# Reading back the reciprocals of a pair of heads: one transfer for both heads, or one transfer per head

## The chip, the cores and the metric

The kernel runs on one core of one Trainium2 chip. The metric is the device time of one execution in microseconds (us); lower is better. The core has a matrix engine (PE in the profile, with its weight loads as PEld), a vector engine (DVE), a scalar engine (ACT), a general engine (POOL) and a sync engine (SP). SP, ACT and POOL can issue DMA transfers; the packets of all transfers are moved by the core's 16 DMA engines.

## The reference

One layer of a streaming encoder over 1024 positions with a width of 1024, all in float32. Two kinds of attention stand side by side, each with 8 heads of 64 columns, and a gated feed-forward block follows. Cut to what matters here:

```python
o_a = from_heads(forgetting_attention(qa, ka, va, log_f))      # 8 heads, strictly causal, with a decay
o_b = from_heads(chunk_band_attention(qc, kc, vc, rel_bias))   # 8 heads, band of 8 chunks back, with a bias
merged = sigmoid(g_A) * (o_a @ w_branch_a) + sigmoid(g_B) * (o_b @ w_branch_b)
x = x + merged @ w_out
x = x + square(relu(rms_norm(x) @ w_up)) @ w_down
return rms_norm(x)
```

Inside both attentions the weights are a softmax: `p = exp(logit - max) / sum(exp(logit - max))`, then `p @ v`. The division by the sum is what this case is about.

## The kernel before, in words

**Stages.** First come the norm and the projections (queries, keys, values and gates; Strassen products of 512-column blocks), to about 430 us of the profile. Then the 16 heads of attention are run one after the other, to about 720 us. Then come the branch products, the output projection, the feed-forward up and down, and the final norm. The matrix engine takes float32 data as a rounded high part and a low part, so that a product is three matmuls; ACT makes the high part, DVE or POOL the low part.

**The attention stage.** The heads are taken in pairs, `pr` = 4, 5, 6, 7 (the forgetting heads), then 0, 1, 2, 3 (the band heads). `hh` is the head within the pair, `h` the half of the 1024 queries. The order of work is written out by hand: strings of letters (`FOX_HEAD`, `BAND_HEAD`, `LAST_HEAD`) name one action each. `S` makes the scores of one block of 128 queries on PE (tile `s`, from the loaded tiles `qk` and `sk`), `R` takes their extremum on DVE (band heads add the loaded bias tile `bc` there), `E` takes the exponential on ACT (tile `p`, with the row sums added up into `den`), `T` turns `p` on PE (`pt`), `H` and `L` make the high and low part (`th` on ACT, `tl` on DVE), `P` multiplies with the loaded values `v` (`pv`), `V` and `X` bring the result out. `F` is one step of a filler: parts of the gated branch products (tile `m`), with weights `wrab`, `wh_ab` and `wl_ab`, which PE runs between attention work in the later heads. `O` and `W`, in the last head alone, split reloaded outputs `olt` (ACT, then DVE) and the first branch weights. The engines' wrappers `TO`, `VO`, `AO` and `LO` keep these instructions in the order of the letters on PE, DVE, ACT and SP; instructions of the bare POOL object `G`, and the bare engines elsewhere, are placed by a planner, which works with modelled times.

**Loads.** All loads of the stage are issued by SP in one order (`LO`). When the scores of a head are done, the tiles `qk` (1 MB) and `sk` (512 KB) of the head after next are loaded into the buffers that this head leaves (`load_head`); `load_bias` and `load_values` do so for `bc` and `v`. So a load has about the time of one head before PE needs it.

**The reciprocals.** The row sums of a pair stand in `den` with one query in each partition. `reciprocals(pr)` inverts them, transposes them in blocks of 32 and writes them to `r_dram[pr]`, a tensor of 2 rows (one for each head) of 1024 floats, in four small transfers. The output tile `on` has the 64 columns of the pair's first head in partitions 0 to 63 and those of the second in partitions 64 to 127, and queries along the free axis. `spread_reciprocals(pr)` therefore reads each row of `r_dram[pr]` into 64 partitions of the tile `rb`, 128 partitions of 4 KB in all, and `normalise` multiplies `on` by `rb`: on POOL (line 860) for seven of the eight pairs, on DVE for the last (pair 3). For the band pairs the product is stored to `o_dram` by SP (the store waits in the list `later` for the next `flush`) and reloaded as `olt`. `spread_reciprocals` is called from `done`, between the two halves of the queries of a pair's second head.

Of the kernel before, what the change touches and what calls it, by code (L numbers as in the profile page):

```python
# [19 lines left out]
S = 1024  # L20
# [3 lines left out]
HD = 64  # L24
# [67 lines left out]
def hybrid_block(ctx: ExitStack, tc: tile.TileContext, xT, xN, g1, wall, wf, fb, relb, g2, g3, outT):  # L92
# [14 lines left out]
    VO, TO, AO, GO, LO = Ordered(V), Ordered(T), Ordered(A), Ordered(G), Ordered(nc.sync)  # L107
# [29 lines left out]
    def dram(name, shape, dt=F32):  # L137
        return dpool.tile(shape, dt, tag=name, name=name)
# [5 lines left out]
    r_dram = dram("r_dram", [8, 2, S])  # L144
# [702 lines left out]

    def spread_reciprocals(pr):
        rb = ap0.tile([P, S], F32, tag="rb", name=f"rb{pr}")
        LO.dma_start(rb, r_dram[pr].rearrange("a (o s) -> a o s", o=1).to_broadcast([2, HD, S]))  # L850
        outs["rb", pr] = rb

    def normalise(pr, h):
# [46 lines left out]
    def done(n, h):  # L900
        pr, hh = HEADS[n]
        flush()
        if n == 15:
            if h == 0:
                spread_reciprocals(pr)
            else:
                normalise(pr, h)
        elif hh:
            if h == 0:
                o = outs[pr, h]  # L910
                G.tensor_tensor(o, o, lows_o[pr], op=ALU.add)
                spread_reciprocals(pr)
            normalise(pr, h)
# [420 lines left out]
```

## Time and profile before

| what | value |
|---|---|
| median of 3 runs | 1477.45 us (1476.58 to 1478.12) |
| the profiled execution | 1475.98 us |
| its span, first to last instruction | 1474.3 us |
| busy: PE, DVE, ACT, POOL | 96%, 60%, 48%, 55% of the span |
| mean granted PE clock | 0.980 |
| data moved by DMA | 259.75 MB, mean 176 GB/s |
| first and last issue of an `rb` transfer | 448.1 us and 697.1 us |

The profile is of one execution. The profile's page gives shares over the whole span; answers for chosen stretches give the busy time of each engine, the granted clock of PE, the share of the 16 DMA engines that was busy and the rate. A wait is put down to what came last, and the chain is followed back from the last instruction to what released each step. The time of a DMA in the chain runs from its issue to its landing.

### The profile page before, as it was taken

The numbers are of one execution on the slowest core, as the hardware profiler recorded it, in microseconds if no ns is written. First come the engines' busy times: TensorE is split into PE (matmuls) and PEld (weight loads), VectorE is DVE, ScalarE is ACT, GpSimd is POOL, SyncE is SP. The second block draws the span as 40 slices with busy tenths as digits, with TensorE's granted clock in tenths as the row PEclk, the third lists the DMA queues.
The fourth block names the chain that finished last, engine by engine and source line by source line (L and its number), as shares of the span: only waits on it lengthen the run. The fifth ranks groups of instructions, "written<-read, shape, count | busy, mean of one in ns | idle before, by whom it ended". The sixth has DMA issues, their size and how long they took to land.

```text
span 1474.3 us, 20382 instructions
## 1 busy us (share of the span) xinstructions
PE 1415.2 (96%) x6658; PEld 1176.5 (80%) x6658; DVE 890.9 (60%) x1385; ACT 707.9 (48%) x1363; POOL 816.0 (55%) x641
## 2 busy tenths in 40 slices
PE   7999999999989888989899999999999999999997
PEld 5788888888877777878688888888888888888886
DVE  7756454533368876656546674555455558999644
ACT  8633333344358776656335443333333444444654
POOL 1477777777802222112453487777776645658463
PEclk9999999999999989989999999999999999999998
DMA  8547667763355576885555334444444875578363
GB/s 275 153 113 199 182 193 216 200 192 133 131 176 157 135 199 172 216 221 194 188 195 169 115 111 147 157 150 157 155 151 139 279 240 173 165 255 222 93 206 123
DMA packets 132580, 259.75 MB, mean 176 GB/s; under 512 B 18354, under 2 KB 20402, under 8 KB 129402
## 3 DMA queue, kind: packets, MB, share of 16 engines
q1 hardware_dynamic: 84618, 173.32, 38.6%
q10 hardware_dynamic: 44656, 77.26, 16.6%
q0 software_dynamic: 3200, 7.88, 2.4%
q8 instruction: 52, 0.85, 0.2%
q14 instruction: 54, 0.44, 0.1%
HBM read 172.70 MB, written 85.69 MB: 175 GB/s over the span
## 4 chain that ended last, share of the span: by engine, by line
PE 73%; DMA 15%; DVE 5%; issue 4%; POOL 1%; ACT 1%; SPq 1%; POOLq 0%; ACTq 0%; DVEq 0%
PE u L215 42%; PE dS L215 8%; PE dA L215 7%; PE o L215 5%; DMA sk<-sk_dram 4%; DMA bc<-relb 3%; PE m L215 3%; PE s L105 2%; DMA rb<-r_dram 2%; PE pv L105 2%; PE pt L105 2%; DMA wr<-wall 2%; DMA xT<-a_dram 1%; DMA v<-v_dram 1%; PE u L105 1%
## 5 line engine op out<-in xcount | busy, mean ns | idle before, releaser
L164 POOL TENSOR_TENSOR wl_A<-wr,wh_A 128x512 fp32r<-128x512 f32 x118 | 157.6, 1345 | 90.2 <-ACT wh_A L162 74.0
L164 POOL TENSOR_TENSOR wl_S<-S,wh_S 128x512 fp32r<-128x512 f32 x102 | 136.5, 1342 | 30.7 <-ACT wh_S L162 30.1
L162 ACT CAST wh_S<-S 128x512 fp32r<-128x512 f32 x105 | 64.7, 621 | 116.9 <-PE u L215 53.7
L105 DVE TENSOR_TENSOR tl<-pt,th 128x512 fp32r<-128x512 f32 (+1 forms) x144 | 90.8, 642 | 31.5 <-ACT th L105 30.0
L162 ACT CAST wh_A<-wr 128x512 fp32r<-128x512 f32 x105 | 64.9, 620 | 86.6 <-PE u L215 47.7
L164 POOL TENSOR_TENSOR wl_S<-ks,wh_S 128x512 fp32r<-128x512 f32 x48 | 70.9, 1565 | 51.9 <-ACT wh_S L105 50.2
L105 ACT CAST th<-pt 128x512 fp32r<-128x512 f32 (+1 forms) x144 | 77.3, 550 | 41.5 <-PE pt L105 39.1
L105 ACT ACTIVATE p<-s,mn 128x640 f32<-128x640 f32 (+3 forms) x120 | 84.2, 702 | 22.0 <-DVE mn L105 21.1
L578 DVE TENSOR_TENSOR u<-u,u 128x512 f32<-128x512 f32 x70 | 48.8, 697 | 74.1 <-PE u L215 71.8
L860 POOL TENSOR_TENSOR on<-on,rb 128x512 f32<-128x512 f32 x14 | 17.7, 1275 | 127.3 <-DMA rb<-r_dram 127.3
L105 PE MATMUL pt<-ident,p 128*128 128x128 f32 x528 | 82.0, 284 | 0.7 <-DVE zt L391 0.6
L185 POOL TENSOR_TENSOR S<-wr,wr 128x512 f32<-128x512 f32 x35 | 46.5, 1328 | 61.1 <-DMA wr<-wall 47.1
L105 PEld LDWEIGHTS pt<-ident,p 128*128 128x128 f32 x528 | 65.0, 146 | 11.2 <-PE pv L105 2.0
L105 PE MATMUL s<-qk 128*128 128x384 f32 (+2 forms) x192 | 60.7, 371 | 13.2 <-DMA qk<-qk_dram 6.6
L105 PE MATMUL s<-sk 96*128 96x384 f32 (+2 forms) x192 | 55.5, 343 | 11.3 <-DMA sk<-sk_dram 11.3
L164 POOL TENSOR_TENSOR wl_A<-ka,wh_A 128x512 fp32r<-128x512 f32 x32 | 46.1, 1449 | 35.2 <-ACT wh_A L105 35.2
L105 PE MATMUL pv<-th,v 128*128 128x512 f32 (+3 forms) x180 | 62.7, 356 | 1.1 <-ACT th L105 0.5
L277 ACT CAST qkh<-qk 128x512 fp32r<-128x512 f32 x32 | 19.9, 621 | 88.4 <-DMA qk_dram<-qkl 34.1
L1089 ACT ACTIVATE v<-v 128x512 f32<-128x512 f32 x64 | 40.4, 632 | 45.3 <-DVE v L1088 43.4
L105 DVE CUSTOM_DVE_ANT_0 s<-s,bc 128x640 f32<-128x640 f32 (+2 forms) x64 | 42.3, 662 | 32.6 <-DMA bc<-relb 18.5
L571 DVE TENSOR_TENSOR u<-u,c 128x512 f32<-128x512 f32 x35 | 24.5, 699 | 55.8 <-PE u L215 53.8
L105 PE MATMUL pv<-tl,v 128*128 128x512 f32 (+3 forms) x180 | 57.7, 339 | 0.2 <-DVE tl L105 0.2
(441 smaller groups left out, 4725.2 us busy)
## 6 DMA issues: line engine op xcount, KB each, us to landing
wr<-wall SPq DMA_DIRECT2D x235, 256.0 KB
a_dram<-at ACTq DMA_DIRECT2D x64, 256.0 KB
xT<-a_dram SPq DMA_DIRECT2D x64, 256.0 KB
qk<-qk_dram SPq DMA_DIRECT2D x15, 1024.0 KB
qk_dram<-qkh ACTq DMA_DIRECT2D x96, 128.0 KB
a_dram<-v ACTq DMA_DIRECT2D x48, 256.0 KB
xB<-a_dram SPq DMA_DIRECT2D x44, 256.0 KB
z_dram<-zt ACTq DMA_DIRECT2D x32, 256.0 KB
```

Source lines behind the costliest of these rows:

```text
L105: return lambda *a, **kw: tc.keep_in_program_order(getattr(self.eng, name)(*a, **kw))
L162: (act.tensor_copy if act is G else act.copy)(wh, src)
L164: lows.append(eng.tensor_tensor(wl, src, wh.bitcast(F32), op=ALU.subtract))
L185: eng.tensor_tensor(t, raw(3), raw(2), op=ALU.add)
L215: done = eng.matmul(bank, w[wi], x[xi], start=(first and t == 0), stop=(t == n - 1 and not part), skip_group_check=part or not first)
L277: A.copy(dst[0], src)
L571: V.tensor_tensor(banks[1], banks[3], c22, op=ALU.add)
L578: V.tensor_tensor(banks[b], banks[b], u2, op=ALU.add)
L860: G.tensor_tensor(o, o, rb, op=ALU.mult)
L1089: A.activation(v, v, AF.Square)
```

## The change

The one transfer that filled all 128 partitions of `rb` becomes two in a loop over the heads of the pair, of 64 partitions each. Source bytes, destination bytes, the issuing queue and the place in SP's order stay the same. The source of the old transfer is a three-dimensional pattern, 2 rows by 64 repeats by 1024 floats; that of each new one is 64 repeats by 1024 floats.

```diff
     def spread_reciprocals(pr):
         rb = ap0.tile([P, S], F32, tag="rb", name=f"rb{pr}")
-        LO.dma_start(rb, r_dram[pr].rearrange("a (o s) -> a o s", o=1).to_broadcast([2, HD, S]))
+        for hh in range(2):
+            LO.dma_start(rb[hh * HD:(hh + 1) * HD, :], r_dram[pr, hh:hh + 1, :].to_broadcast([HD, S]))
         outs["rb", pr] = rb
```

## The prediction

> **What bounds the kernel now.** I read the page first: the busy times, the chain, the group of line 860.
>
> ```profile
> PE 1415.2 (96%) x6658; PEld 1176.5 (80%) x6658; DVE 890.9 (60%) x1385; ACT 707.9 (48%) x1363; POOL 816.0 (55%) x641
> PE 73%; DMA 15%; DVE 5%; issue 4%; POOL 1%; ACT 1%; SPq 1%; POOLq 0%; ACTq 0%; DVEq 0%
> L860 POOL TENSOR_TENSOR on<-on,rb 128x512 f32<-128x512 f32 x14 | 17.7, 1275 | 127.3 <-DMA rb<-r_dram 127.3
> ```
>
> PE is busy for 96% of the span, so a gain must come out of its 59 us of idle time or out of a slowed clock. The chain holds 15% of DMA. POOL waits 127.3 us for `rb`, seven times, 18 us each: for 512 KB that is long. Next, the chain in order of time, which gives the transfers of the attention stage from issue to landing, and the PE stretch that follows the stage:
>
> ```profile
> 452.75 16.50 DMA sk<-sk_dram
> 484.00 17.43 DMA sk<-sk_dram
> 550.13 21.04 DMA sk<-sk_dram
> 625.67 17.06 DMA rb<-r_dram
> 715.99 39.05 PE m L215 x163
> ```
>
> The `sk` load issued at 452.75 needs 16.5 us, though only one `rb` transfer (448.05) stands ahead of it and its neighbours. Why is seen in busy time by windows, whose last columns are the PE clock, the share of the 16 DMA engines and the rate:
>
> ```profile
> 449.10:452.10 3.00, 3.00 (x17) 2.56 (x16) 2.84 (x8) 2.00 (x5) 0.00 (x0) 1.00 0.12 46
> 452.90:460.00 7.10, 6.40 (x46) 5.71 (x46) 5.99 (x16) 6.66 (x16) 0.00 (x0) 1.00 0.95 237
> 462.80:464.00 1.20, 1.20 (x8) 0.97 (x8) 1.20 (x4) 1.19 (x3) 0.00 (x0) 1.00 0.14 48
> 584.90:587.00 2.10, 2.10 (x16) 1.96 (x15) 1.88 (x5) 1.37 (x3) 0.00 (x0) 1.00 0.10 29
> 676.00:679.00 3.00, 3.00 (x20) 2.64 (x18) 2.78 (x7) 2.15 (x6) 0.00 (x0) 1.00 0.14 55
> ```
>
> While `rb` is alone in flight (first row), 0.12 of 16 engines are busy: two, at 23 GB/s each. With the loads behind it, all are busy (0.95). By 462.8 the share is back at 0.14, while `sk` lands at 469.25: the other 14 engines have done their part, and the load waits for its share on the two that still carry `rb`. The last two rows show the same in other pairs. So each `rb` transfer makes two engines late by 7 to 10 us, and everything issued behind it is as late as they are.
>
> [...]
>
> What this costs PE: its waits in the stage, then the stretches that hold them (engine columns PE, PEld, DVE, ACT, POOL), and last the sum of the eight stretches between these.
>
> ```profile
> PE s L105 <- DMA sk<-sk_dram: 11.3, 6, 2.3
> PE s L105 <- DMA qk<-qk_dram: 6.6, 4, 3.4
> PE m L215 <- ACT wh_ab L105: 5.2, 1, 5.2
> PE m L105 <- POOL wl_ab L745: 5.1, 3, 4.2
> PE pv L105 <- DMA v<-v_dram: 0.5, 1, 0.5
> ```
>
> ```profile
> 467.16:474.14 6.98, 4.74 (x24) 4.08 (x24) 4.14 (x15) 3.95 (x11) 3.50 (x4) 0.76 0.94 262
> 498.19:504.87 6.68, 3.61 (x16) 3.53 (x17) 2.85 (x9) 3.37 (x8) 4.51 (x5) 0.74 0.94 256
> 530.14:542.41 12.27, 8.06 (x31) 7.12 (x32) 5.15 (x16) 5.33 (x14) 6.78 (x7) 0.58 0.72 200
> 565.35:576.54 11.19, 5.62 (x16) 4.54 (x17) 2.03 (x5) 2.30 (x7) 7.29 (x7) 0.70 0.80 241
> 607.30:612.10 4.80, 2.75 (x14) 1.99 (x13) 0.76 (x3) 1.54 (x5) 0.84 (x1) 1.00 0.99 320
> 642.40:655.05 12.65, 6.40 (x17) 4.81 (x17) 2.24 (x6) 2.61 (x7) 4.98 (x4) 0.60 0.72 245
> 709.40:719.90 10.50, 5.15 (x12) 3.64 (x12) 5.02 (x5) 3.38 (x6) 4.66 (x3) 0.68 0.39 124
> sum 65.07, PE 36.33 PEld 29.70 DVE 22.19 ACT 22.48 POOL 32.56; mean PE 5.19 PEld 4.24 DVE 3.17 ACT 3.21 POOL 4.65
> ...
> sum 206.08, PE 202.24 PEld 175.50 DVE 159.34 ACT 152.65 POOL 27.43; mean PE 25.28 PEld 21.94 DVE 19.92 ACT 19.08 POOL 3.43
> ```
>
> Seven stretches, one near the end of each head or pair that has an `rb` transfer in flight, hold 65.07 us with only 36.33 us of PE work. And the clock falls: 0.58 to 0.76 in six of the seven, which are those with the longest waits, against 1.00 in the one with short waits. Between them PE is busy 202.24 of 206.08 us, 98.1%, at full clock.
>
> **The change, part by part.** *More engines.* Each half has 64 rows of 4 KB, four per engine if it uses 16. At the 23 GB/s per engine of the lone transfer, 512 KB on 16 engines take 1.4 us; at the full load's 237 GB/s, 2.2 us. A fixed part comes on top, for which this row of the chain, a write of 2 KB, gives a bound of 2.8 us:
>
> ```profile
> 622.70 2.83 DMA r_dram<-rt
> ```
>
> So `rb` lands 4 to 5 us after its issue instead of 16 to 17 (up to 8 where loads stand ahead). POOL's waits fall from 127.3 us to 7 x 5 = 35, which is worth nothing in itself except where POOL delays PE. Loads behind it lose the wait for two late engines and pay at most 2.2 us for the bytes that now go over their engines too. `sk` of the first pair, issued at 452.75, should land by 462, when the other engines were done (0.14 at 462.8); PE wants it at 467.16, 5 us later. That margin is the cover of the remaining cost.
>
> *One more issue.* Eight more DMA instructions on SP, each new one priced by loads of 64 rows:
>
> ```profile
> L105 SPq DMA_DIRECT2D rb<-r_dram x8: 533/540/578, 448.1 to 697.1; - x8
> L105 SPq DMA_DIRECT2D sk<-sk_dram x12: 455/465/1442, 452.8 to 651.9; - x12
> L105 SPq DMA_DIRECT2D bc<-relb x16: 465/578/963, 515.8 to 653.2; - x16
> ```
>
> Two issues of 0.46 to 0.58 instead of one of 0.54 add 0.4 to 0.6 us per pair, 3 to 5 us on SP in all. In the first pair the next issues come at 452, 3.4 us after `rb`, and hide it. Where loads follow at once (the last pair's `olt`), they go out 0.5 us later, and land earlier all the same. Without that cover it would be 8 x 0.5 = 4 us; I take 0.3 us per pair, 2.4. POOL waits for two transfers instead of one; the second wait costs one semaphore check, 17 ns by this row, eight times, under other waiting:
>
> ```profile
> L860 POOLq EVENT_SEMAPHORE  x8: 17/17/17, 464.1 to 680.8; - x8
> SPq L105 <- POOL on L860: 38.8, 3, 13.2
> ACT oh L105 <- DMA olt<-o_dram: 11.1, 1, 11.1
> ```
>
> *What moves with it.* SP stands 38.8 us behind line 860 for the stores to `o_dram`, with weight loads queued behind them. POOL waits for `rb` ahead of `wl_ab`, for which PE then waits 4.2 us. In the last head ACT waits 11.1 us for `olt`, issued right behind `rb`, and `wh_ab`, for which PE waits 5.2 us, stands behind that on ACT. All three shrink with `rb`.
>
> *The sum.* Idle time in the seven stretches: 65.07 - 36.33 = 28.7 us. Clock: the lost share, (1 - clock), times the length of each sums to 20.4 us; times PE's busy time instead to 11.4. Slow clock over idle time costs nothing, over work everything; I take the middle, 15.9. The work of these stretches at full clock is then 36.33 - 15.9 = 20.4 us, and at the 98.1% of the other stretches 20.8. Upper bound of the saving: 65.07 - 20.8 = 44.3.
>
> Next late: ACT. The first three pair periods and a wait-free stretch:
>
> ```profile
> 448.05:479.80 31.75, 28.81 (x173) 24.91 (x174) 25.62 (x59) 25.85 (x61) 7.61 (x7) 0.95 0.57 151
> 479.80:511.70 31.90, 28.14 (x171) 24.67 (x169) 25.11 (x58) 25.22 (x59) 7.59 (x7) 0.95 0.57 150
> 511.70:546.47 34.77, 29.87 (x166) 25.76 (x164) 24.66 (x57) 24.79 (x57) 9.39 (x9) 0.85 0.65 167
> 474.14:498.19 24.05, 23.37 (x146) 20.12 (x144) 20.76 (x43) 21.18 (x48) 3.07 (x3) 1.00 0.47 122
> ```
>
> ACT has 75.9 us of work in these three pairs. Bound by PE alone they would take some 82 us, with ACT at 92%; its best sustained share here is 21.18 of 24.05, 88%, which gives 86.2. That takes 4.1 back. 44.3 - 4.1 - 2.4 = 37.8 us. The profiled execution took 1475.98, 1.5 below the median of the runs: 1476.0 - 37.8 = 1438.
>
> It reaches the end, because the stretch after the stage is PE work without a gap (39.05 us in the chain) and later weight loads start when buffers come free, earlier too.
>
> **The rivals.** *Part of it only.* The waits for `sk`, `qk` and `v` go (11.3 + 6.6 + 0.5 = 18.4) but the clock stays as it is, ACT takes its 4.1 and SP 2.4: 12 us, 1464; with a third of the rest about 1455. For it: the reason for the slow clock is seen only by its place beside the waits. Against: 1.00 in the one stretch whose waits are short.
>
> *No gain.* Two halves are two transfers over the same engines with the fixed part paid twice, and what PE waits for is late for another reason: 1476, or 1480 with all of SP's 4 us. Against: engines stand idle (0.14) while `sk` is awaited. [...]
>
> [...]
>
> *Slower by the source row.* Sixteen engines read one row of 4 KB at once. If a row gives its 23 GB/s however many read it, a half takes 11.4 us, both 22.8 one after the other, with all engines held: everything behind lands 9 us later than now, in six places about 54 us, 1530. It decides where both halves need over 16.5 us, below 38 GB/s from one row. For it: nothing here reads a row with 16 engines. Against: one engine's 23 GB/s on one row is above the 15 GB/s (237 / 16) that each gets under full load, so the row is not what limits.
>
> **How the numbers follow.** Forecast 0.74, part of it 0.14, no gain 0.06, no change from two engines 0.01, and slower 0.05 (source row 0.03, one engine 0.02). The forecast alone spans 1427 (the clock's upper bound, 20.4, and nothing taken back: 65.07 - 15.9 / 0.981 = 48.9) to 1450. Down to 1428 and up to 1463, which takes in most of "part of it", leaves out about 2 in 10. Measurements tell some 0.2%, 3 us, from no change: faster 0.88, same 0.07, slower 0.05.
>
> **What would show it.** Right: with `rb` alone in flight the DMA share is near 0.9 for 2 us instead of 0.12; line 860 waits some 35 us in place of 127; `sk` lands 8 to 9 us after issue; the clock keeps 1.00 through most of the stage; PE's waits for `qk` and `sk` nearly vanish; the stage ends 35 to 40 us sooner and the rest has its old length. Wrong: a share of 0.06 or 0.12 again, or waits of PE on ACT that grow by as much as the DMA waits shrink.

## The result, and the profile after

The changed kernel takes 1433.28 us (median) against 1477.78 us before, a ratio of 0.9695 (95% interval 0.9675 to 0.9714). Measured again with another set of runs it takes 1432.24 against 1478.67 us, 0.9681 (0.9657 to 0.9705). That is 44.5 and 46.4 us saved, where 38 were forecast. In the profiled execution of the first measurement, one of the four runs in the 1433.28, PE was slow from end to end (7217 us), so every line of "after" below comes from the second measurement, whose profiled span is 1430.6 us.

The page after, in the lines that answer to those of before (busy times; the chain; and, from the list of all groups of instructions, POOL's multiplication, now on line 861):

```profile
PE 1397.9 (98%) x6658; PEld 1165.7 (81%) x6658; DVE 884.8 (62%) x1385; ACT 706.5 (49%) x1363; POOL 813.5 (57%) x641
PE 83%; issue 4%; DVE 4%; POOL 3%; ACT 2%; DMA 2%; SPq 0%; POOLq 0%; ACTq 0%; DVEq 0%
L861 POOL TENSOR_TENSOR on<-on,rb 128x512 f32<-128x512 f32 x14 | 17.8, 1287 | 42.0 <-DMA rb<-r_dram 42.0
```

DMA's part in the chain falls from 15% to 2%. Between 440 and 760 us the DMA steps of 16 to 21 us quoted before are gone: the chain there is PE work for 93%, and no DMA stands in it. POOL waits 42.0 us for `rb` where it waited 127.3, 6 us each.

Busy time by windows: `rb` alone in flight, the loads behind it, and the time in which before only two engines were left at work.

```profile
450.60:452.40 1.80, 1.80 (x10) 1.50 (x9) 1.80 (x4) 0.85 (x4) 0.00 (x0) 1.00 0.97 250
454.40:461.00 6.60, 5.91 (x43) 5.19 (x42) 5.29 (x15) 6.18 (x17) 6.09 (x6) 1.00 0.94 299
463.00:465.00 2.00, 2.00 (x14) 1.73 (x13) 2.00 (x5) 1.99 (x6) 0.00 (x0) 1.00 0.00 0
```

The share of the 16 DMA engines (last column but one) is 0.97 where it was 0.12, and by 463 us, where two engines went on alone before, nothing is left to move.

The traces also note the landing of each transfer in 16 parts. Six `sk` loads of the stage are issued right behind an `rb` transfer. Before, 14 of the 16 parts of such a load were there 8.6 to 11.5 us after its issue, and the last two came 7.5 to 12 us later, so that the load landed after 16.5 to 22.1 us. Now all 16 parts are there after 7.3 to 9.3 us in four of the six and after 11.0 and 12.9 us in the other two (8 to 9 were forecast). That a part is one engine's share is the author's reading; it agrees with two late parts at a share of 0.12 here and four at 0.26 in the run on four engines below.

All waits of PE in the attention stage, in sum, times, and the longest:

```profile
PE s L105 <- ACT p L105: 5.7, 9, 0.9
PE s L105 <- DVE tl L105: 0.2, 1, 0.2
```

The waits for `sk`, `qk`, `wh_ab`, `wl_ab` and `v` are all gone. Last, the attention stage as a whole, from the first `rb` issue to the start of the last high part of `o3h`, before and then after, in one row each:

```profile
448.05:719.90 271.85, 238.59 (x1360) 205.23 (x1361) 182.22 (x403) 175.65 (x403) 60.63 (x52) 0.92 0.66 183
```

```profile
449.22:676.50 227.28, 221.41 (x1358) 193.92 (x1357) 180.79 (x402) 174.19 (x402) 61.11 (x52) 1.00 0.74 219
```

PE has the same work. Its idle time falls from 33.3 to 5.9 us (271.85 - 238.59, 227.28 - 221.41), which gives 27.4 us; its busy time falls by 17.2 us because the granted clock is 1.00 in place of 0.92. Together 44.6 us. (The stage begins 1.2 us later than before, so the span is shorter by 43.7 us.) Behind the stage nothing changes: 1474.3 - 719.90 = 754.4 us before, 1430.6 - 676.50 = 754.1 after. On PE, DVE and POOL the instructions stand in the same order in both traces, and SP has eight issues more.

### The profile page after: what moved, and what is told of

Read it like the earlier page. It is cut to its first block, busy times and chain, and to the rows that moved or that the text cites. A ratio compares the mean times of both kernels' runs of the same rounds, so it can differ in the third digit from the quotient of the medians.

```text
span 7216.0 us, 20385 instructions
## 1 busy us (share of the span) xinstructions
PE 7199.5 (100%) x6658; PEld 4883.8 (68%) x6658; DVE 888.7 (12%) x1385; ACT 725.0 (10%) x1363; POOL 787.4 (11%) x641
## 4 chain that ended last, share of the span: by engine, by line
PE 100%; DVE 0%; DMA 0%; ACT 0%; SPq 0%; issue 0%; DVEq 0%
PE u L215 51%; PE dS L215 9%; PE o L215 7%; PE dA L215 6%; PE s L105 5%; PE pt L105 5%; PE pv L105 5%; PE m L105 4%; PE m L215 4%; PE g L362 2%; PE u L105 1%; PE dA L105 1%; PE f L374 1%; PE vtp L615 1%; PE n_b L105 0%; PE n_b L248 0%
## 5 line engine op out<-in xcount | busy, mean ns | idle before, releaser
L105 PE MATMUL pt<-ident,p 128*128 128x128 f32 x528 | 393.9, 1040 | 0.0
L215 PE MATMUL u<-B11h,wh_A 128*128 128x512 f32 x140 | 233.9, 1671 | 0.0
L215 PE MATMUL u<-T2h,wh_S 128*128 128x512 f32 x140 | 230.9, 1649 | 0.0
L215 PE MATMUL u<-T2l,wh_S 128*128 128x512 f32 x140 | 230.1, 1644 | 0.0
L215 PE MATMUL u<-B11l,wh_A 128*128 128x512 f32 x140 | 230.1, 1643 | 0.0
L215 PE MATMUL u<-T2h,wl_S 128*128 128x512 f32 x140 | 230.1, 1643 | 0.0
L215 PE MATMUL u<-B11h,wl_A 128*128 128x512 f32 x140 | 229.6, 1640 | 0.0
L215 PE MATMUL u<-B21h,wh_A 128*128 128x512 f32 x136 | 224.1, 1648 | 0.0
L215 PE MATMUL u<-B21l,wh_A 128*128 128x512 f32 x136 | 223.7, 1645 | 0.0
L215 PE MATMUL u<-T1l,wh_S 128*128 128x512 f32 x136 | 223.7, 1645 | 0.0
```

The lines of the kernel that those rows point to most:

```text
L105: return lambda *a, **kw: tc.keep_in_program_order(getattr(self.eng, name)(*a, **kw))
L215: done = eng.matmul(bank, w[wi], x[xi], start=(first and t == 0), stop=(t == n - 1 and not part), skip_group_check=part or not first)
```

## The experiments

The theory: the old transfer runs on two engines (0.12 of 16), because the slowest dimension of its source is 2; all that is issued behind it waits for these two. The main rival: having two transfers is what helps.

**Two transfers, still on two engines.** Against the changed kernel:

```diff
-            LO.dma_start(rb[hh * HD:(hh + 1) * HD, :], r_dram[pr, hh:hh + 1, :].to_broadcast([HD, S]))
+            LO.dma_start(rb[hh * HD:(hh + 1) * HD, :], r_dram[pr, hh:hh + 1, :].rearrange("a (o s) -> a o s", o=1).to_broadcast([2, HD // 2, S]))
```

> Two transfers of 64 rows each as in the change, but with the source written as 2 repeats of 32 repeats of the row, so that its slowest dimension is 2. Theory (the number of engines is set by the slowest dimension, and two late engines are the whole cost): each half uses two engines, lands after 12 to 17 us, and nothing is gained: 1474 to 1481 us, ratio 0.998 to 1.003. Rival (the split into two transfers is what helps): 1433 us.

Measured: 1490.82 us, ratio 1.0078 (1.0048 to 1.0108). The rival falls: two transfers on two engines gain nothing. The expectation of no change missed too, by 10 us. Windows with the halves alone in flight, then the longest waits of the SP queue, then PE's:

```profile
450.20:453.20 3.00, 3.00 (x17) 2.45 (x15) 2.84 (x6) 1.99 (x5) 0.00 (x0) 1.00 0.13 33
483.40:487.20 3.80, 3.80 (x21) 3.24 (x21) 3.80 (x8) 2.80 (x8) 0.00 (x0) 1.00 0.13 38
```

```profile
SPq L105 <- DMA rb<-r_dram: 20.8, 4, 7.2
```

```profile
PE s L105 <- DMA qk<-qk_dram: 20.9, 5, 9.2
PE s L105 <- DMA sk<-sk_dram: 10.6, 6, 2.2
```

The share, 0.13, says two engines. But they move 33 to 38 GB/s where the old transfer's two moved 46. SP now also waits 20.8 us for landings of `rb` before it issues later loads, and PE's wait for `qk` grows from 6.6 to 20.9 us. Why the two engines are slower than before is taken up below.

**The change itself again, one transfer on 16 engines, and none.** The second takes the first head's row for both heads, the third loads `rb` for the first pair alone. The lines below stand in place of the old transfer, the first line for the second kernel, the rest for the third.

```diff
+        LO.dma_start(rb, r_dram[pr, 0:1, :].to_broadcast([P, S]))
...
+        if pr == 4:
+            rb = outs["rb"] = ap0.tile([P, S], F32, tag="rb", name=f"rb{pr}")
+            for hh in range(2):
+                LO.dma_start(rb[hh * HD:(hh + 1) * HD, :], r_dram[pr, hh:hh + 1, :].to_broadcast([HD, S]))
+        outs["rb", pr] = outs["rb"]
```

> The changed kernel once more, for a trace at full clock (the profiled execution of the first measurement took 7217 us, with PE slow throughout). Theory (two late engines): about 1433 us; each half lands on 16 engines some 3 to 5 us after its issue, `sk` 8 to 9 us after issue instead of 16 to 21; line 860 waits some 35 us instead of 127; PE's waits for `sk` and `qk` nearly vanish and the clock stays at 1.00 from 448 us to the end of the attention stage. Rival (the split itself helps: POOL can start on one half sooner, or SP's order shifts): `sk` would still need 16 us, and the gain would show as PE waiting less for POOL alone.

> One transfer of 128 rows, the source a plain repeat of the first head's row 128 times; the second head's reciprocals are left out, so its rows are divided by the wrong sums. Theory (number of engines): as fast as the change, 1431 to 1435 us, by up to 3 us faster for eight issues less on SP. Rival (the split helps): 1476 us as before. Rival (16 engines on one row are slow): `rb` lands later than in the change, because 128 instead of 64 reads go to one row.

> The transfer of the changed form is made for the first pair only; the other seven pairs use its values, so their reciprocals are left out. This bounds what is left to gain in the transfer. Theory: the change already hides it, so 1429 to 1434 us, at most 4 us below the change. Rival (the remaining 7 transfers still delay the loads behind them by some 2 us each): 1420 us or less.

Measured, against the same runs of before: the change 1432.24 us (0.9681), one transfer 1433.87 us (0.9694, 0.9663 to 0.9725), first pair alone 1432.21 us (0.9684, 0.9655 to 0.9713). One transfer on 16 engines is as good as two, within 2 us, so the split has no worth of its own; it is only the way by which the source's slowest dimension becomes 64. Without seven of the eight transfers nothing more is gained: the change takes all that this read can give. The single transfer with `rb` alone in flight:

```profile
450.20:451.70 1.50, 1.50 (x9) 1.28 (x8) 1.50 (x5) 1.37 (x4) 0.00 (x0) 1.00 0.83 314
```

314 GB/s out of one row of 4 KB, at a share of 0.83: the rival by which the source row limits the rate falls.

**Four and eight engines.** The kernel of the first experiment with `[4, HD // 4, S]` and `[8, HD // 8, S]`.

> As the kernel with two halves on two engines each, but with the source written as 4 repeats of 16 repeats of the row. Theory (the slowest dimension sets the engines): four engines; they get 128 KB each, at 23 GB/s 5.7 us, so both halves land some 8 to 10 us after issue, and `sk` some 11 to 12 us after its own, still ahead of PE's need in the early pairs (some 14 us): most of the gain, 1434 to 1446 us. Rival (only 16 engines avoid the waits, or the pattern's form and not the count is what costs): 1470 us or more.

> As before with 8 repeats of 8 repeats of the row. Theory: eight engines, 64 KB each, landing 5 to 6 us after issue, no load late for PE: 1431 to 1436 us, as the change. Rival (every engine short of 16 delays loads): halfway between four engines and the change.

Measured: four engines 1464.84 us, ratio 0.9900 (0.9882 to 0.9917); eight engines 1438.05 us, 0.9722 (0.9698 to 0.9747). With `rb` alone in flight, four engines and then eight:

```profile
451.80:454.60 2.80, 2.80 (x14) 2.37 (x13) 2.64 (x7) 1.80 (x5) 0.00 (x0) 1.00 0.26 64
```

```profile
449.30:451.30 2.00, 2.00 (x11) 1.69 (x10) 2.00 (x5) 1.22 (x3) 0.00 (x0) 1.00 0.47 129
```

The share is 0.26 and 0.47, four engines and eight, as 0.13 was two: in these windows of the first pair the number of engines is that of the slowest dimension. (With four, a window of the next pair, 481.0 to 483.2 us, has a share of 0.14 at 58 GB/s; no run explains it.) All three patterns of 2, 4 and 8 repeats have the same form, so it is the count that costs, and not the form. Eight give nearly the whole gain: the interval, 1434 to 1441 us by the ratio, reaches into the expected 1431 to 1436, and whether the last few us are lost is not settled; halfway to four engines, as the rival had it, would be 1449. Four missed the expectation by 19 us: each engine moves 16 GB/s (64 / 4), not the 23 that the sum went by, so `rb` is whole 11 to 15 us after the first issue (8 to 10 were expected) and the `sk` loads behind it land after 14.9 to 20.2 us (11 to 12 were expected), too late for PE:

```profile
PE s L105 <- DMA sk<-sk_dram: 10.2, 6, 2.3
PE s L105 <- DMA qk<-qk_dram: 6.4, 3, 2.8
PE m L215 <- ACT wh_ab L105: 1.7, 1, 1.7
```

The waits for `sk` and `qk` stand as before the change, those behind POOL and `olt` are nearly gone.

**The old transfer on ACT's queue.** `LO.dma_start` becomes `AO.dma_start`, nothing else.

> The transfer of before, one for both heads on two engines, issued by ACT at the same place of the order instead of by SP. Theory (what hurts PE is that the loads' shares stand behind `rb` in SP's rows of the two engines): on another queue the two engines alternate between `rb` and the loads, so `qk` and `sk` land some 11 to 13 us after issue and PE mostly doesn't wait, while `rb` itself lands no sooner; the waits of PE for `wl_ab` (4.2 us) stay: 1440 to 1455 us. Rival (the two engines are short of rate, whatever the queue): the waits stay as they are, 1472 to 1480 us, or above by ACT's eight issues.

Measured: 1489.69 us, ratio 1.0076 (1.0056 to 1.0096). The time missed the expectation by 35 us. The waits:

```profile
POOL on L860 <- DMA rb<-r_dram: 139.1, 7, 22.1
ACT th L105 <- DMA r_dram<-rt: 19.9, 4, 6.5
PE s L105 <- ACT p L105: 19.3, 11, 5.5
PE pt L105 <- DVE tl L105: 9.5, 4, 3.9
PE m L105 <- POOL wl_ab L745: 7.0, 1, 7.0
PE m L215 <- ACT o3h L105: 5.4, 1, 5.4
PE s L105 <- POOL sk L480: 3.2, 1, 3.2
```

PE waits for no load of `sk` or `qk` any more (the 3.2 us are for a fill of `sk` on POOL). The loads are not on time, though. The last two parts of the six `sk` loads behind `rb` still come late, and the loads land 13.0 to 14.9 us after issue: 2.4 to 9.1 us sooner than before, when they stood behind `rb` in SP's queue, but not at the 7.3 to 12.9 us of the change. So the place in SP's queue accounts for some of the lateness, and the rest comes on the two engines that the loads share with `rb`; that these alternate between the queues, as the expectation had it, was not shown. PE is also held up elsewhere in this run, and how much of the vanished waits is owed to that was not separated. The read must also wait until `r_dram` is written, which SP can afford and ACT can't: ACT stands 19.9 us for it, and PE waits for ACT's exponentials and high parts instead. That was not in the expectation.

**The change in the forgetting pairs alone.** A condition `pr >= 4` chooses the two halves, the old transfer stays for the band pairs.

> The change in pairs 4 to 7 alone, the old transfer in the four band pairs. Theory: the gain is the sum over pairs. The stretches of the first four pairs hold 37.1 of the 65.1 us with late loads and 22.0 of 36.3 us of PE work; from their idle time (15.1) and their share of the slow clock they give some 22 to 25 us: 1452 to 1457 us. Rival (waits removed early come back in the band pairs, where DMA is busier): under 18 us gained, or the gain of the whole within 5 us.

Measured: 1457.62 us, ratio 0.9853 (0.9836 to 0.9869), 21 us gained, 0.6 us outside what was expected. By subtraction the band pairs give the other 23 to 25; a kernel with the change in them alone was not run. Little comes back later. Of PE's waits for DMA and POOL, and for `wh_ab`, only those of the band pairs are left, and they hold 16.1 us where they held 13.7 before:

```profile
PE m L105 <- POOL wl_ab L745: 8.0, 3, 3.9
PE s L105 <- ACT p L105: 5.6, 9, 0.9
PE m L215 <- ACT wh_ab L105: 4.7, 1, 4.7
PE s L105 <- DMA sk<-sk_dram: 3.4, 2, 2.0
```

**Even and odd partitions.** Why do two engines move 33 to 38 GB/s in the first experiment? Each transfer reads one row, and the old one read two. And if each engine takes one index of the slowest dimension, which the author assumed and no trace shows, they write partitions 0 to 31 and 32 to 63 of a transfer, and in the old transfer partitions 64 apart. Filling the even partitions by the one transfer and the odd ones by the other keeps the single row and the two transfers, and by that assumption puts the engines 64 partitions apart. The second kernel does it with 16 engines. Each line stands in place of the transfer of the changed kernel.

```diff
+            LO.dma_start(rb[hh:P:2, :], r_dram[pr, hh:hh + 1, :].rearrange("a (o s) -> a o s", o=1).to_broadcast([2, HD // 2, S]))
...
+            LO.dma_start(rb[hh:P:2, :], r_dram[pr, hh:hh + 1, :].to_broadcast([HD, S]))
```

> Two transfers on two engines each, as the kernel that took 1490.8 us, but one fills the even and the other the odd partitions of `rb`, so that the two engines of a transfer write partitions 64 apart instead of 32 apart; the heads' reciprocals are mixed up. Theory (two engines that write partitions 32 apart get in each other's way, which is why that kernel was slower than before): alone in flight the two engines move some 45 to 50 GB/s as in the kernel before, not 33 to 38, and the time is 1475 to 1483 us. Rival (reading the same row with two engines, or having two transfers, is what slowed them): 33 to 38 GB/s again and 1488 to 1493 us.

> The change with the same even and odd partitions, 16 engines. Theory: each transfer now reaches all 128 partitions' range, so that `rb` alone in flight moves some 300 GB/s, as in the one transfer of 128 rows, instead of 225 to 250, and lands 0.5 us sooner; the time stays at 1430 to 1436 us, because nothing waits for it. Rival (the rate is that of two transfers): 225 to 250 GB/s.

Measured: on two engines 1472.37 us, ratio 0.9951 (0.9935 to 0.9967), on 16 engines 1432.19 us, 0.9678 (0.9662 to 0.9694). `rb` alone in flight, two engines and then 16:

```profile
449.50:452.00 2.50, 2.50 (x14) 2.11 (x12) 2.34 (x6) 1.55 (x4) 0.00 (x0) 1.00 0.13 49
```

```profile
450.30:452.00 1.70, 1.70 (x10) 1.44 (x9) 1.70 (x3) 1.23 (x3) 0.00 (x0) 1.00 0.79 275
```

The two engines are back at 49 GB/s, so it was the partitions that a transfer fills, and neither the single row nor the number of transfers. The 16 engines move 275 GB/s at a share of 0.79: more than the change's 250 at 0.97, less than the 300 that was expected, and worth nothing in time, as expected. The kernel on two engines came out 3 us below its expectation and 8 below the 1480.05 us of the kernel before, measured beside it. Its `rb` is whole 0.3 to 1.9 us sooner, and PE's waits for `qk` and `wh_ab` are shorter (4.3 and 3.8 us instead of 6.6 and 5.2), those for `sk` longer (12.3 instead of 11.3); that this is the whole of it was not tested.

## Why the prediction was right

*Two engines.* Right, at every count tried: shares of 0.12, 0.26, 0.47 and 0.97 for a slowest dimension of 2, 4, 8 and 64. That 64 repeats would take 16 engines, on which the forecast rests, no row of before showed; with the change the share was 0.97. One transfer is as good as two when it uses 16 engines (1433.87 us, at a share of 0.83).

*All that is issued behind them is late.* Right: of each `sk` load behind `rb`, two of the 16 parts were late, by 7.5 to 12 us (7 to 10 in the prediction). With four engines four parts were, 14.6 us and more after issue against 11.9 at most for the other twelve (first pair). The queue is one reason and not the only one: with the transfer on ACT's queue PE waits for no load of `sk` or `qk`, yet these `sk` loads land 0.9 to 7.4 us later than with the change.

*What moves with it.* Right: SP stands 4.5 us behind POOL's multiplication in place of 38.8, ACT 3.0 us for `olt` in place of 11.1, and PE no longer for `wl_ab` and `wh_ab`.

*The idle time.* 28.7 us were forecast in the seven stretches; 27.4 went in the whole stage, with 5.9 left, nearly all of it for ACT. *The clock.* 15.9 us were taken as the middle of 11.4 and 20.4; it was 17.2. The clock needs no cause of its own: where PE's waits went, it stood at 1.00, which the rival "part of it only" denied.

*What was taken back.* Here the sum was off. The upper bound of 44.3 us was nearly the result; 4.1 us for ACT and 2.4 for SP were taken off it. SP's term is nothing: one issue less per pair gains nothing (1433.87 against 1432.24). ACT's term was right in its place and too large for the stage:

```profile
449.22:478.48 29.26, 27.77 (x175) 23.87 (x174) 25.77 (x60) 25.99 (x60) 7.64 (x7) 1.00 0.58 164
478.48:505.31 26.83, 25.39 (x160) 21.91 (x158) 23.34 (x55) 23.61 (x55) 7.59 (x7) 1.00 0.60 178
505.31:534.97 29.66, 28.13 (x178) 24.15 (x177) 26.19 (x62) 26.40 (x62) 9.55 (x10) 1.00 0.72 202
```

The first three pairs take 85.75 us (86.2 forecast), with ACT at 76.0 of them, 89%, and PE at 81.29, 94.8%. At 98.1% these would be 82.9 us, so ACT took back 2.9. PE's own waits for ACT grew by 1.1 us only, from 4.6 to 5.7. And the rest of the stage ran above the 98.1%: PE 140.12 of 141.53 us, 99.0%, which gave 1.3 back. In the whole stage 1.6 us were lost against 98.1% (227.28 - 221.41 / 0.981), not 6.5. These 4.9 us and the 1.3 of the clock bring 37.8 to 44.0, and so account for nearly all of the difference.

*`rb` itself.* POOL's waits fell to 42.0 us, 35 were forecast. Counted from the first issue of a pair, `rb` is whole after 4.4 to 4.9 us in six pairs and 7.6 in two, as forecast (4 to 5, up to 8 with loads ahead). POOL's wait, 6.0 us on average, was forecast at 5; it counts from when POOL is free, which in five of the seven pairs is before SP issues the transfer. Before the change `rb` took 13.2 to 19.9 us, a wider range than the 16 to 17 of the prediction.

## What to carry to other kernels

Read the DMA share where a transfer is alone in flight: here it told two engines (0.12), four (0.26) and eight (0.47) from 16 (0.79 to 0.97). A transfer of 512 KB at 0.12 made the loads issued behind it on its queue late here (`sk` landed after 16.5 to 22.1 us, with the change after 7.3 to 12.9), with 14 engines free. Look at the slowest dimension of a broadcast's source: for 64 partitions, 2 repeats outermost ran on two engines (0.13) and 64 on all 16 (0.97), as did 128 for 128 partitions (0.83). Eight engines were nearly enough (1438.05 us), four were not (1464.84), and whether it takes one transfer or two was of no weight (1433.87 and 1432.24). Price a late load by the clock too: here the slow clock after the waits cost 17 us beside the 27 of the waits themselves.

## What the runs showed that was not expected

*The partitions that a transfer fills matter.* On two engines, a transfer into every second of 128 partitions moves 49 GB/s, and one into 64 neighbouring partitions 33 to 38; four engines get 64 GB/s into 64 neighbouring partitions, 16 each. By the author's assumption above, the two engines write 64 partitions apart in the first and 32 apart in the second; why the rates differ was not shown.

*A slow clock came after two microseconds of waiting.* In the kernel before, PE waits 2.2 us for `sk`, and 1.3 us after it goes on the granted clock is 0.50 for 3.4 us (a PE row, with its wait in brackets, and a window). It need not come: with the old transfer on ACT's queue a gap of 2.7 us at 447.3 us was followed by no slow clock until 483 us, where it came after a gap of 3.9. What sets it was not shown.

```profile
469.39 0.30 PE L105 MATMUL s<-sk 96*128 96x128 f32 x1 [2.23 <-DMA sk<-sk_dram]
```

```profile
470.73:474.14 3.41, 3.40 (x13) 2.70 (x12) 2.80 (x10) 1.85 (x8) 0.07 (x1) 0.50 1.02 209
```
